# Attention values as 128-column float32r matmuls, with the mask and the row maximum in one operation

## The chip, the cores and the metric

The kernel runs on one core of one Trainium2 chip. The metric is the device time of one execution in microseconds (us). The profiler calls the engines PE (TensorE: matmuls; its weight loads are listed apart as PEld), DVE (VectorE), ACT (ScalarE), POOL (GpSimd) and SP (SyncE, which issues the large DMAs).

## The reference

One decoder layer on x of 256 tokens by 1024 features, all float32. The part that the change touches is the attention: 8 heads of 64 features, one block of 256 tokens, so that the block-sparse attention of the reference is plain causal attention.

```python
h = rmsnorm(x, norm_mix_g)
q, k, v, u_pool, gate_logits = split(h @ w_in)
q, k = rotary(rmsnorm(heads(q))), rotary(rmsnorm(heads(k)))
p = softmax(where(k_pos <= q_pos, q @ k.T * Dh ** -0.5, -1e30))
attn = p @ v
mixed = sigmoid(gates[0]) * (attn @ w_branch_attn) + sigmoid(gates[1]) * (pooled @ w_branch_pool)
x = x + mixed @ w_out
x = x + ffn(rmsnorm(x))        # up projection, causal convolution, silu(gate) * value, down projection
```

## The kernel before

**Float32 from two halves.** Nearly every product runs as three float32r matmuls. An operand is split into a high part (`high`, a ScalarE copy to float32r) and a low part (`low`, VectorE: the operand less its high part), and `mm3` (L95 to L101) multiplies high by high, high by low and low by high into one PSUM accumulator. Weights arrive as raw chunks of 128 x 2048 by DMA and are split in pieces of 128 x 1024: `next_high` and `next_low`, called by `ahead`, keep ScalarE and VectorE some pieces ahead of PE. The tiles of a split chunk are named after what they belong to: `hi_g`, `lo_g` for the gates, `bp` and `ba` for the two branch weights, `o` for the output weights.

**Order of the work.** The instructions of each engine run in the order in which the program writes them; the end of the program ties them to it. The stages, as PE sees them: q, k and v (to 38 us), the four pool inputs `ps_u`, sixteen gate tiles n = 0 to 15 (`ps_g`, 24 matmuls each), eight tiles j = 0 to 7 of the pool branch (`ps_bp`, 12 matmuls each), eight tiles of the attention branch (`ps_ba`), the output projection, and the feed-forward part from 144 us on. After each gate tile, and after every second tile of the pool branch (j = 1, 3, 5, 7), a `tick` advances a clock, and functions that were put off with `later(n, ...)` run n ticks on. Behind the tick come `ahead` and the tile's eviction by VectorE (L559 for a gate, L582 for the pool branch), so anything a tick adds on VectorE or ScalarE stands in front of the eviction.

**The attention.** It is done for pairs of heads, hp = 0 to 3, between the gate tiles. `scores` runs before the gate tiles 1, 5, 9 and 13: four float32 matmuls into a PSUM tile of three blocks of 128 columns per head (the first 128 queries with the first 128 keys, and the other 128 queries with all 256), one VectorE operation that adds the mask (L480), two reductions for the maxima (L484), one that scales them (L485), four exponentials with sums on ScalarE (L492), a reciprocal (L495), two multiplications on GpSimd (L498). Four ticks on, `weigh` transposes the weights on PE (L506) and copies them out (`pT`, L508). Four ticks later (one for the last pair) `values` multiplies: eight matmul records per pair, float32, 64 stationary columns of v each, into `ps_o` (L517); ScalarE and VectorE split the result into `ath` and `atl` (L519, L520). So the tick behind gate tile 8 runs the values of pair 0 and the transposes of pair 1; behind gate tile 12 the values of pair 1 and the transposes of pair 2; behind tile 1 of the pool branch the values of pair 2 and the transposes of pair 3; behind tile 3 the values of pair 3. Before gate tile 10 the pool maps `ps_m` run.

**Buffers.** The eight PSUM banks are four single ones (`mm`: gate tiles, branch tiles, `ps_o`) and two pairs (`ps2`: scores, transposes, pool maps). A new tile gets the slot that was given back first, and its first matmul waits for the last reader of the tile that was there. `vn` (v by token) lies in the same buffer as the tokens that the first norm reads.

Of the kernel before, what the change touches and what calls it, by code (L numbers as in the profile page):

```python
# [8 lines left out]
F32 = mybir.dt.float32  # L9
F32R = mybir.dt.float32r  # L10
AF = mybir.ActivationFunctionType
ALU = mybir.AluOpType
AX = mybir.AxisListType

P = 128
S = 256
NT = S // P
D = 1024
KD = D // P
H = 8  # L20
DH = 64
AW = H * DH
KA = AW // P
# [6 lines left out]
HALF = ROPE // 2  # L30
EPS = 1e-6
NEG = -1e30
CH = 2048


# [31 lines left out]
def hybrid_layer_kernel(ctx: ExitStack, tc: tile.TileContext, xq_d, xtok_d, par_d, wkv_d, wpg_d,  # L67
                        wpool_d, wba_d, wbp_d, wout_d, wup_d, wdn_d, out_d):
    nc = tc.nc

    const = ctx.enter_context(tc.tile_pool(name="const", bufs=1))
# [3 lines left out]
    act = ctx.enter_context(tc.tile_pool(name="act", bufs=1))  # L75
# [4 lines left out]
    tmp = mixer.enter_context(tc.tile_pool(name="tmp", bufs=2))  # L80
# [5 lines left out]
    def high(hi, src, scale=1.0):  # L86
        nc.scalar.activation(hi, src, AF.Copy, scale=scale)  # L87

    def low(lo, hi, src, scale=None):
        if scale is None:  # L90
            nc.vector.tensor_tensor(lo, src, hi.bitcast(F32), ALU.subtract)  # L91
        else:
            nc.vector.scalar_tensor_tensor(lo, src, scale, hi.bitcast(F32), ALU.mult, ALU.subtract)
# [24 lines left out]
    def load(parts=1):  # L118
# [5 lines left out]
        n = src.shape[-1]  # L124
        raws[c] = raw_p.tile([P, CH], F32, tag="raw", name=f"raw_{name}{c}")
        for i in range(parts):
# [8 lines left out]
    for c, (name, src) in enumerate(order):  # L135
        n = CH if name == "q" else src.shape[-1]
        parts = 4 if name == "q" else 2 if n == CH else 1
        pieces += [(c, slice(i * n // parts, (i + 1) * n // parts), i == 0, i == parts - 1) for i in range(parts)]
# [5 lines left out]
    at = [0, 0]  # L144
# [8 lines left out]
    def next_high():  # L153
        if at[0] < len(pieces):
# [4 lines left out]
            if first:  # L159
                moving = order[c][0] in "qkv"  # L160
                place = MOVING if moving else 0
                his[c] = whi_p.tile([P, CH + P], F32R, tag="whi", name=f"hi_{order[c][0]}{c}")[:, place:]
                place = MOVING if moving else FAR
                los[c] = wlo_p.tile([P, CH + P], F32R, tag="wlo", name=f"lo_{order[c][0]}{c}")[:, place:]
            high(his[c][:, sl], raw(c, sl))
# [13 lines left out]
    def ahead(upto=0):  # L179

        next_high()
        next_low()
        if at[1] - sum(p[0] < used[0] for p in pieces) < upto:
            next_high()
            next_low()
# [29 lines left out]
    load(2)  # L215
    load()

    vn = act.tile([P, 2 * NT, AW], F32, tag="v", name="vn")
    xtok = vn.rearrange("p (t a) b -> p t (a b)", t=NT)
    nc.sync.dma_start(out=xtok, in_=xtok_d)  # L220
    nc.sync.dma_start(out=par, in_=par_d)
    for _ in range(RAWBUFS - 2):
# [4 lines left out]
    for i in range(WARM):  # L227
# [6 lines left out]
    nc.gpsimd.memset(eps, EPS)  # L234
    mhalf = const.tile([P, H], F32, name="mhalf")
    nc.gpsimd.memset(mhalf, -0.5)
    mask = const.tile([P, 3, P], F32, name="mask")
    nc.gpsimd.memset(mask, 0.0)
    nc.gpsimd.affine_select(out=mask[:, 0:3:2, :], in_=mask[:, 0:3:2, :], compare_op=ALU.is_ge, fill=NEG,
                            base=0, pattern=[[0, 2], [-1, P]], channel_multiplier=1)  # L240
    rcnt = const.tile([P, 16], F32, name="rcnt")
    nc.gpsimd.iota(rcnt, pattern=[[1, 16]], base=1, channel_multiplier=0,
                   allow_small_or_imprecise_dtypes=True)
# [142 lines left out]
    ptq = project("q", on_q)  # L386
    ptk = project("k", on_k)

    psv = ps2.tile([P, 2, 512], F32, tag="ps2", name="ps_v")
    ptv = project("v", on_v, [psv[:, t, :] for t in range(NT)])  # L390
    for t in range(NT):
# [5 lines left out]
    def later(n, fn, *args):  # L397
        due.setdefault(clock[0] + n, []).append((fn, args))
# [43 lines left out]
    for b in range(2):  # L442
        w = chunk("p")
        for c in range(2):
            ps = feature_tile(w, c, f"u{b}{c}")
# [9 lines left out]
                    nc.gpsimd.tensor_tensor(qs[:, t, :], qs[:, t, :], mhalf[:, 0:H], ALU.pow)  # L455


    ath = act.tile([P, KA, S], F32R, tag="ath", name="ath")
    atl = act.tile([P, KA, S], F32R, tag="atl", name="atl")
    gates = xq[:, :, S:].rearrange("p k (i s) -> p k i s", s=S)  # L460

    def gate(n):
# [4 lines left out]
    TOK = (slice(0, P), slice(P, 3 * P))  # L467

    def scores(hp):
        ps = ps2.tile([P, 2, 512], F32, tag="ps2", name=f"ps_s{hp}")  # L470
        for j in range(2):
            rows = slice(j * DH, (j + 1) * DH)
            nc.tensor.matmul(ps[:, j, P:3 * P], qT[rows, hp, P:S], kT[rows, hp, :], start=True, stop=True)
            nc.tensor.matmul(ps[:, j, 0:P], qT[rows, hp, 0:P], kT[rows, hp, 0:P], start=True, stop=True)
        if hp == 0:

            for _ in range(2):
                next_high()
        sm = tmp.tile([P, 2, 3 * P], F32, tag="big", bufs=4, name=f"sm{hp}")
        nc.vector.tensor_tensor(sm, ps[:, :, 0:3 * P],  # L480
                                mask.rearrange("p a b -> p (a b)")[:, None, :].to_broadcast([P, 2, 3 * P]), ALU.add)
        mx = tmp.tile([P, 2, 2], F32, tag="mx", name=f"mx{hp}")
        for t in (1, 0):
            nc.vector.tensor_reduce(mx[:, t, :], sm[:, :, TOK[t]], axis=AX.X, op=ALU.max)  # L484
        nc.vector.scalar_tensor_tensor(mx, mx, -1.0, qs[:, :, 2 * hp:2 * hp + 2], ALU.mult, ALU.mult)  # L485
        if hp == 0:
            for _ in range(2):
                next_low()
        sums = tmp.tile([P, 2, 2], F32, tag="sums", name=f"sums{hp}")
        for j in range(2):  # L490
            for t in (1, 0):
                nc.scalar.activation(sm[:, j, TOK[t]], sm[:, j, TOK[t]], AF.Exp, bias=mx[:, t, j:j + 1],  # L492
                                     scale=qs[:, t, 2 * hp + j:2 * hp + j + 1], accum_out=sums[:, t, j:j + 1])
        rs = tmp.tile([P, 2, 2], F32, tag="rs", name=f"rs{hp}")
        nc.vector.reciprocal(rs, sums)  # L495
        for t in (1, 0):
            n = TOK[t].stop - TOK[t].start
            nc.gpsimd.tensor_tensor(sm[:, :, TOK[t]], sm[:, :, TOK[t]],  # L498
                                    rs[:, t, :, None].to_broadcast([P, 2, n]), ALU.mult)
        later(4, weigh, hp, sm)  # L500

    def weigh(hp, sm):
        pp = ps2.tile([P, 2, 512], F32, tag="ps2", name=f"ps_p{hp}")
        for j in range(2):
            for b in range(3):
                nc.tensor.transpose(pp[:, j, b * P:(b + 1) * P], sm[:, j, b * P:(b + 1) * P], ident)  # L506
        pT = tmp.tile([P, 2, 3 * P], F32, tag="big", bufs=4, name=f"pT{hp}")
        nc.scalar.activation(pT, pp[:, :, 0:3 * P], AF.Copy)  # L508
        later(1 if hp == KA - 1 else 4, values, hp, pT)

    def values(hp, pT):

        po = bank(f"ps_o{hp}")
        for b in range(2):
            for j in range(2):
                h = 2 * hp + j
                nc.tensor.matmul(po[j * DH:(j + 1) * DH, b * P:S], vn[:, b, h * DH:(h + 1) * DH],  # L517
                                 pT[:, j, 2 * b * P:(2 * b + 2 - b) * P], start=b == 0, stop=b == 1)
        high(ath[:, hp, :], po[:, 0:S])  # L519
        low(atl[:, hp, :], ath[:, hp, :], po[:, 0:S])  # L520

    waiting = list(range(KD, 2 * KD)) + list(range(KD))

# [23 lines left out]
    for n in range(2 * KD):  # L547
        if n >= FIRST and (n - FIRST) % 4 == 0:
            scores((n - FIRST) // 4)
        if n == 10:  # L550
            pool_maps()
            ahead()
        b, c = n // 2, n % 2
        if c == 0:
            w = chunk("g")
        ps = feature_tile(w, c, f"g{n}")
        tick()
        ahead(AHEAD if n % 2 else 0)
        nc.vector.tensor_tensor(gate(n), ps[:, 0:S], R1, ALU.mult)  # L559
        if n >= 2 * KD - 2:  # L560
            sigmoids(3)


    def branch(src, oph, opl, j, w):
        hi, lo = w
        ps = bank(f"ps_b{src}{j}")
        for k in range(4):
            sl = slice(k * 512 + (j % 4) * P, k * 512 + (j % 4 + 1) * P)
            mm3(ps[:, 0:S], (hi[:, sl], lo[:, sl]), (oph[:, k, :], opl[:, k, :]), k == 0, k == 3)
        return ps  # L570

    for j in range(KD):
        if j % 4 == 0:
            w = chunk("bp")
        ps = branch("p", poolh, pooll, j, w)
# [8 lines left out]
    tmp = ctx.enter_context(tc.tile_pool(name="ffn", bufs=2))  # L584
# [3 lines left out]
    for j in range(KD):  # L588
        if j % 4 == 0:
            w = chunk("ba")  # L590
        ps = branch("a", ath, atl, j, w)
        sigmoids(1)
        if j in (1, 3):
            ahead()
        nc.vector.tensor_tensor(gate(j), ps[:, 0:S], gate(j), ALU.mult)
        nc.gpsimd.tensor_tensor(gate(j), gate(j), gate(KD + j), ALU.add)
        high(mh[:, j, :], gate(j))
        if j:
            low(ml[:, j - 1, :], mh[:, j - 1, :], gate(j - 1))
# [39 lines left out]
    for b in range(4):  # L639
        w = chunk("o")  # L640
        ps = [bank(f"ps_out{b}{c}") for c in range(2)]
# [92 lines left out]
    w = chunk("up")  # L734
    ps = [bank("ps_up1_0")]
# [6 lines left out]
    for i in range(1, KF):  # L742
        if i > 1:
            w = chunk("up")
            ps = [up_tile(w, 0, i)]
# [101 lines left out]
```

## Time and profile before

| what | value |
|---|---|
| three runs | 335.17, 335.31, 335.36 us |
| span of the profiled execution, first to last instruction | 333.6 us |
| what lies around the span, against the median of the runs | 1.7 us |
| granted TensorE clock, mean | 0.998 |
| PE busy | 328.6 us (99%) |
| VectorE busy | 254.9 us (76%) |
| ScalarE busy | 202.6 us (61%) |
| GpSimd busy | 82.3 us (25%) |

The profile is of one execution. Times inside it count from its first instruction. A row of the timeline has the start, the length, the engine, the line in the kernel, the operation and what it writes and reads; in square brackets stands how long the engine was idle before it, and who ended that. The chain of waits is followed back from the last instruction; its rows have a start, a length and what ran. The lengths of matmuls overlap, so their spacing is taken from the chain or from counts in a stretch of time. A row of the stretches has the length, then each engine's busy time with its number of instructions.

### The profile page before, as it was taken

The page shows a single profiled execution, that of the slowest core. Times are in us where ns is not written, and L with a number is a line of the kernel's source. Part 1 is how long each engine was busy: PE and PEld are TensorE (multiplying, and loading weights), DVE is VectorE, ACT ScalarE, POOL GpSimd, SP SyncE. Part 2 cuts the span into 40 slices and gives each one's busy share as a digit, 9 for nine tenths or more (in the row PEclk, how much of TensorE's full clock was granted, in tenths as well). Part 3 has the DMA queues.
Part 4 walks back from the last instruction along what each step waited for, and adds up shares of the span by engine and source line. Part 5 has one row for each costly group of instructions (what it writes and reads, how often), then busy time and mean ns, then how long its engine had stood idle before and what let it go on. Part 6 is the DMA issues. An engine that isn't in the chain of part 4 may idle for free.

```text
span 333.6 us, 6696 instructions
## 1 busy us (share of the span) xinstructions
PE 328.6 (99%) x2728; PEld 319.5 (96%) x2728; DVE 254.9 (76%) x408; ACT 202.6 (61%) x326; POOL 82.3 (25%) x98
## 2 busy tenths in 40 slices
PE   8999999999999999999999999999999999999995
PEld 7888899999999999999999999999999999999995
DVE  4939979979778866877997977777777777768844
ACT  5767626645849945767766766555656464646520
POOL 1007771102404034121241212121212121221330
PEclk9999999999999999999999999999999999999999
DMA  7999763474455660763529283636454555543003
GB/s 266 422 415 205 226 271 129 157 253 149 145 210 181 218 235 2 252 210 110 209 106 358 72 328 129 252 130 252 140 240 146 233 163 216 182 198 128 0 2 126
DMA packets 11102, 63.94 MB, mean 192 GB/s; under 512 B 1472, under 2 KB 2752, under 8 KB 4032
## 3 DMA queue, kind: packets, MB, share of 16 engines
q1 hardware_dynamic: 10656, 63.39, 53.3%
q8 instruction: 21, 0.34, 0.4%
q10 hardware_dynamic: 416, 0.13, 0.3%
q14 instruction: 9, 0.07, 0.1%
HBM read 62.47 MB, written 1.05 MB: 190 GB/s over the span
## 4 chain that ended last, share of the span: by engine, by line
PE 97%; DMA 1%; ACT 0%; DVE 0%; issue 0%
PE ps_up L99 12%; PE ps_up L101 12%; PE ps_up L100 12%; PE ps_d L707 6%; PE ps_d L709 6%; PE ps_d L708 6%; PE ps_g L99 5%; PE ps_g L101 4%; PE ps_g L100 4%; PE ps_q L298 3%; PE ps_k L298 3%; PE ps_v L298 3%; PE ps_out L99 2%; PE ps_out L101 2%; PE ps_out L100 2%; DMA xq<-in_xq 1%
## 5 line engine op out<-in xcount | busy, mean ns | idle before, releaser
L101 PE MATMUL ps_up<-hhi,lo_up 128*128 128x256 f32 x352 | 97.2, 276 | 0.0
L99 PE MATMUL ps_up<-hhi,hi_up 128*128 128x256 f32 x352 | 97.2, 276 | 0.0
L100 PE MATMUL ps_up<-hlo,hi_up 128*128 128x256 f32 x352 | 97.2, 276 | 0.0
L100 PEld LDWEIGHTS ps_up<-hlo,hi_up 128*128 128x128 f32 x352 | 66.1, 188 | 0.0
L101 PEld LDWEIGHTS ps_up<-hhi,lo_up 128*128 128x128 f32 x352 | 66.1, 188 | 0.0
L99 PEld LDWEIGHTS ps_up<-hhi,hi_up 128*128 128x128 f32 x352 | 66.1, 188 | 0.0
L91 DVE TENSOR_TENSOR lo_up<-raw_up,hi_up 128x1024 fp32r<-128x1024 f32 x44 | 54.7, 1261 | 7.3 <-ACT hi_up L87 7.3
L707 PE MATMUL ps_d<-ah,hi_dn 128*128 128x256 f32 x176 | 48.6, 276 | 0.0
L708 PE MATMUL ps_d<-al,hi_dn 128*128 128x256 f32 x176 | 48.6, 276 | 0.0
L709 PE MATMUL ps_d<-ah,lo_dn 128*128 128x256 f32 x176 | 48.6, 276 | 0.0
L689 POOL TENSOR_TENSOR c_v<-c_g,c_v 128x256 f32<-128x256 f32 x22 | 16.2, 736 | 121.4 <-DVE c_v L672 121.4
L87 ACT ACTIVATE hi_up<-raw_up 128x1024 fp32r<-128x1024 f32 x44 | 44.1, 1047 | 0.0
L87 ACT ACTIVATE ah<-c_v 128x256 fp32r<-128x256 f32 x22 | 9.2, 418 | 45.6 <-POOL c_v L689 45.6
L99 PE MATMUL ps_g<-xhi,hi_g 128*128 128x256 f32 x128 | 35.9, 280 | 0.0
L100 PE MATMUL ps_g<-xlo,hi_g 128*128 128x256 f32 x128 | 35.3, 276 | 0.0
L101 PE MATMUL ps_g<-xhi,lo_g 128*128 128x256 f32 x128 | 35.3, 276 | 0.0
L707 PEld LDWEIGHTS ps_d<-ah,hi_dn 128*128 128x128 f32 x176 | 33.0, 188 | 0.0
L708 PEld LDWEIGHTS ps_d<-al,hi_dn 128*128 128x128 f32 x176 | 33.0, 188 | 0.0
L709 PEld LDWEIGHTS ps_d<-ah,lo_dn 128*128 128x128 f32 x176 | 33.0, 188 | 0.0
L91 DVE TENSOR_TENSOR lo_dn<-raw_dn,hi_dn 128x1024 fp32r<-128x1024 f32 x22 | 27.8, 1263 | 0.4 <-ACT hi_dn L87 0.4
L677 DVE TENSOR_TENSOR u_v<-ps_up,R 128x256 f32<-128x256 f32 x22 | 9.3, 421 | 20.9 <-PE ps_up L101 20.8
L714 POOL TENSOR_TENSOR al<-c_v,ah 128x256 fp32r<-128x256 f32 x22 | 22.0, 1002 | 11.6 <-ACT ah L87 11.6
(188 smaller groups left out, 794.7 us busy)
## 6 DMA issues: line engine op xcount, KB each, us to landing
raw_up<-in_wup SPq DMA_DIRECT2D x22, 1024.0 KB, 4.9
raw_dn<-in_wdn SPq DMA_DIRECT2D x11, 1024.0 KB, 4.9
raw_g<-in_wpg SPq DMA_DIRECT2D x8, 1024.0 KB, 5.9
raw_o<-in_wout SPq DMA_DIRECT2D x4, 1024.0 KB, 4.7
raw_v<-in_wkv SPq DMA_DIRECT2D x2, 1024.0 KB, 15.4
raw_p<-in_wpg SPq DMA_DIRECT2D x2, 1024.0 KB, 12.9
raw_bp<-in_wbp SPq DMA_DIRECT2D x2, 1024.0 KB, 4.8
raw_ba<-in_wba SPq DMA_DIRECT2D x2, 1024.0 KB, 4.7
```

The lines of the kernel that those rows point to most:

```text
L87: nc.scalar.activation(hi, src, AF.Copy, scale=scale)
L91: nc.vector.tensor_tensor(lo, src, hi.bitcast(F32), ALU.subtract)
L99: nc.tensor.matmul(out, sh, mh, start=start, stop=False, **kw)
L100: nc.tensor.matmul(out, sh, ml, start=False, stop=False, **kw)
L101: nc.tensor.matmul(out, sl, mh, start=False, stop=stop, **kw)
L298: nc.tensor.matmul(pt[t], sx[:, k, t * P:(t + 1) * P], wx[:, sl], start=k == 0 and sx is xhi and wx is hi, stop=k == KD - 1 and wx is lo)
L677: nc.vector.tensor_tensor(u, ps[:, 0:S], R2, ALU.mult)
L689: nc.gpsimd.tensor_tensor(uc[1], g[1], uc[1], ALU.mult)
L707: nc.tensor.matmul(o, hi[:, sl], acch[i], start=first, stop=False, skip_group_check=True)
L708: nc.tensor.matmul(o, hi[:, sl], accl[i], start=False, stop=False, skip_group_check=True)
L709: nc.tensor.matmul(o, lo[:, sl], acch[i], start=False, stop=i == KF - 1, skip_group_check=True)
L714: nc.gpsimd.tensor_tensor(accl[i], act_i, acch[i].bitcast(F32), ALU.subtract)
```

## The change

**Values.** v is split once into high and low parts in float32r (`part_values`, before gate tile 7): for each pair of heads `vv` holds the four blocks high and low of the first head, low and high of the second. The transposed weights are split too: `ph` by ScalarE out of PSUM, `pl` by VectorE, one tick after the transposes (at once for the last pair). Eight float32r matmuls per pair then have 128 stationary columns, the high and the low part of one head side by side, and add up all four products; a head's two halves of PSUM are summed afterwards: ScalarE copies one half out, and `joined`, one tick later (at once for the last pair), adds the other on VectorE, and splits the sum by a ScalarE copy and a subtraction on GpSimd. The copies and sums of all pairs use one buffer. `vn` lies in the buffer that the split attention result takes later.

**Scores.** Four fused operations (add the mask, maximum along the row) take the place of the mask addition and the two reductions. The mask shrinks to two blocks.

```diff
+    vn = act.tile([P, NT, AW], F32, tag="ath", name="vn")
+    vv = act.tile([P, NT, KA, 4, DH], F32R, tag="v", name="vv")
...
+    def part_values():
+        for t in range(NT):
+            v4 = vn[:, t, :].rearrange("p (q j d) -> p q j d", j=2, d=DH)
+            high(vv[:, t, :, 0:4:3, :], v4)
+            for j in range(2):
+                low(vv[:, t, :, 1 + j, :], vv[:, t, :, 3 * j, :], v4[:, :, j, :])
+        heads.extend(act.tile([P, KA, S], F32R, tag=tag, name=tag) for tag in ("ath", "atl"))
...
-        nc.vector.tensor_tensor(sm, ps[:, :, 0:3 * P],
-                                mask.rearrange("p a b -> p (a b)")[:, None, :].to_broadcast([P, 2, 3 * P]), ALU.add)
         mx = tmp.tile([P, 2, 2], F32, tag="mx", name=f"mx{hp}")
-        for t in (1, 0):
-            nc.vector.tensor_reduce(mx[:, t, :], sm[:, :, TOK[t]], axis=AX.X, op=ALU.max)
+        masks = (mask[:, 1, :], mask.rearrange("p a b -> p (a b)"))
+        for j in range(2):
+            for t in (1, 0):
+                nc.vector.tensor_tensor_reduce(sm[:, j, TOK[t]], ps[:, j, TOK[t]], masks[t], 1.0, LOWEST,
+                                               ALU.add, ALU.max, mx[:, t, j:j + 1])
...
-        pT = tmp.tile([P, 2, 3 * P], F32, tag="big", bufs=4, name=f"pT{hp}")
-        nc.scalar.activation(pT, pp[:, :, 0:3 * P], AF.Copy)
-        later(1 if hp == KA - 1 else 4, values, hp, pT)
+        ph = tmp.tile([P, 2, 3 * P], F32R, tag="big", bufs=4, name=f"ph{hp}")
+        pl = tmp.tile([P, 2, 3 * P], F32R, tag="big", bufs=4, name=f"pl{hp}")
+        high(ph, pp[:, :, 0:3 * P])
+        if hp == KA - 1:
+            low(pl, ph, pp[:, :, 0:3 * P])
+        else:
+            later(1, low, pl, ph, pp[:, :, 0:3 * P])
+        later(1 if hp == KA - 1 else 4, values, hp, ph, pl)
...
-        for b in range(2):
-            for j in range(2):
-                h = 2 * hp + j
-                nc.tensor.matmul(po[j * DH:(j + 1) * DH, b * P:S], vn[:, b, h * DH:(h + 1) * DH],
-                                 pT[:, j, 2 * b * P:(2 * b + 2 - b) * P], start=b == 0, stop=b == 1)
-        high(ath[:, hp, :], po[:, 0:S])
-        low(atl[:, hp, :], ath[:, hp, :], po[:, 0:S])
+        for j in range(2):
+            for p in (ph, pl):
+                for b in range(2):
+                    nc.tensor.matmul(po[:, j * S + b * P:(j + 1) * S],
+                                     vv[:, b, hp, 2 * j:2 * j + 2, :].rearrange("p a d -> p (a d)"),
+                                     p[:, j, 2 * b * P:(2 * b + 2 - b) * P], start=j == 0 and p is ph and b == 0,
+                                     stop=p is pl and b == 1, skip_group_check=True)
+        sums = tmp.tile([P, 2, S], F32, tag="q2", bufs=1, name=f"at{hp}")
+        for j in range(2):
+            nc.scalar.activation(sums[halves[j], 0, :], po[halves[1 - j], j * S:(j + 1) * S], AF.Copy)
+        if hp == KA - 1:
+            joined(hp, po, sums)
+        else:
+            later(1, joined, hp, po, sums)
+
+    def joined(hp, po, sums):
+        for j in range(2):
+            nc.vector.tensor_tensor(sums[halves[j], 1, :], po[halves[j], j * S:(j + 1) * S], sums[halves[j], 0, :], ALU.add)
+        high(heads[0][:, hp, :], sums[:, 1, :])
+        nc.gpsimd.tensor_tensor(heads[1][:, hp, :], sums[:, 1, :], heads[0][:, hp, :].bitcast(F32), ALU.subtract)
...
+        if n == 7:
+            part_values()
```

More of the change, by code (lines that the diff above doesn't have):

```diff
@@ L32 @@
 NEG = -1e30
+LOWEST = -3e38
 CH = 2048
@@ L216, in hybrid_layer_kernel @@
     load()
-    vn = act.tile([P, 2 * NT, AW], F32, tag="v", name="vn")
-    xtok = vn.rearrange("p (t a) b -> p t (a b)", t=NT)
+    xtok = act.tile([P, NT, D], F32, tag="v", name="xtok")
     nc.sync.dma_start(out=xtok, in_=xtok_d)
@@ L236, in hybrid_layer_kernel @@
     nc.gpsimd.memset(mhalf, -0.5)
-    mask = const.tile([P, 3, P], F32, name="mask")
+    mask = const.tile([P, 2, P], F32, name="mask")
     nc.gpsimd.memset(mask, 0.0)
-    nc.gpsimd.affine_select(out=mask[:, 0:3:2, :], in_=mask[:, 0:3:2, :], compare_op=ALU.is_ge, fill=NEG,
-                            base=0, pattern=[[0, 2], [-1, P]], channel_multiplier=1)
+    nc.gpsimd.affine_select(out=mask[:, 1, :], in_=mask[:, 1, :], compare_op=ALU.is_ge, fill=NEG,
+                            base=0, pattern=[[-1, P]], channel_multiplier=1)
     rcnt = const.tile([P, 16], F32, name="rcnt")
@@ L455, in hybrid_layer_kernel @@
                     nc.gpsimd.tensor_tensor(qs[:, t, :], qs[:, t, :], mhalf[:, 0:H], ALU.pow)
-    ath = act.tile([P, KA, S], F32R, tag="ath", name="ath")
-    atl = act.tile([P, KA, S], F32R, tag="atl", name="atl")
+    heads = []
+    def part_values():
[5 more added lines that the diff above has]
+        heads.extend(act.tile([P, KA, S], F32R, tag=tag, name=tag) for tag in ("ath", "atl"))
     gates = xq[:, :, S:].rearrange("p k (i s) -> p k i s", s=S)
@@ L506, in weigh @@
                 nc.tensor.transpose(pp[:, j, b * P:(b + 1) * P], sm[:, j, b * P:(b + 1) * P], ident)
-        pT = tmp.tile([P, 2, 3 * P], F32, tag="big", bufs=4, name=f"pT{hp}")
-        nc.scalar.activation(pT, pp[:, :, 0:3 * P], AF.Copy)
-        later(1 if hp == KA - 1 else 4, values, hp, pT)
-    def values(hp, pT):
-        po = bank(f"ps_o{hp}")
-        for b in range(2):
-            for j in range(2):
-                h = 2 * hp + j
-                nc.tensor.matmul(po[j * DH:(j + 1) * DH, b * P:S], vn[:, b, h * DH:(h + 1) * DH],
-                                 pT[:, j, 2 * b * P:(2 * b + 2 - b) * P], start=b == 0, stop=b == 1)
-        high(ath[:, hp, :], po[:, 0:S])
-        low(atl[:, hp, :], ath[:, hp, :], po[:, 0:S])
+        ph = tmp.tile([P, 2, 3 * P], F32R, tag="big", bufs=4, name=f"ph{hp}")
@@ new lines, in weigh, with values @@
+        pl = tmp.tile([P, 2, 3 * P], F32R, tag="big", bufs=4, name=f"pl{hp}")
[5 more added lines that the diff above has]
+        later(1 if hp == KA - 1 else 4, values, hp, ph, pl)
+    halves = (slice(0, DH), slice(DH, P))
+    def values(hp, ph, pl):
+        po = bank(f"ps_o{hp}")
+        for j in range(2):
[12 more added lines that the diff above has]
+            later(1, joined, hp, po, sums)
@@ L590, in hybrid_layer_kernel @@
             w = chunk("ba")
-        ps = branch("a", ath, atl, j, w)
+        ps = branch("a", heads[0], heads[1], j, w)
         sigmoids(1)
```

## The prediction

> **What bounds the kernel now.** I read the page's busy times first, then the chain that ended last, then the list of what PE waited for, and last the three queues (PE, VectorE, ScalarE) around the four head pairs. All times are us.
>
> ```profile
> span 333.6 us, 6696 instructions
> PE 328.6 (99%) x2728; PEld 319.5 (96%) x2728; DVE 254.9 (76%) x408; ACT 202.6 (61%) x326; POOL 82.3 (25%) x98
> PE 97%; DMA 1%; ACT 0%; DVE 0%; issue 0%
> ...
> PE ps_warm L228 <- DVE ones L196: 1.1, 1, 1.1
> PE ps_q L298 <- ACT hi_q L87: 0.4, 1, 0.4
> ...
> 55.00:65.00 10.00, 10.00 (x90) 10.00 (x89) 9.75 (x20) 6.10 (x14) 1.64 (x2) 1.00 0.27 71
> 104.00:117.00 13.00, 13.00 (x116) 12.11 (x115) 10.99 (x18) 12.99 (x25) 0.64 (x1) 1.00 0.74 253
> ```
>
> PE is the bound, and after its first 6 us it waits for nothing: its only two waits are at the start. So every microsecond in which PE is made to wait later is added to the end, and nothing after it can give it back. The windows also show where that is easy: from 104 to 117, the stage of the pool branch (`ps_bp`), ScalarE is busy 12.99 of 13.00 and VectorE 10.99, against 6.10 and 9.75 of 10.00 in the gate stage (this one is columns PE, PEld, DVE, ACT, POOL, clock, DMA). The clock is full in both. The 90 matmuls of 10.00 us in the gate stage, nearly all float32r with 256 moving columns, are 0.111 apart; twelve of them, one tile of the pool branch, take some 1.38 (four such tiles lie between 111.96 and 117.5 below).
>
> The four head pairs in the chain of waits (start, length):
>
> ```profile
> 65.74 0.66 PE ps_p L506 x6
> ...
> 78.37 0.80 PE ps_o L517 x8
> 79.17 0.81 PE ps_p L506 x6
> ...
> 107.62 0.81 PE ps_p L506 x6
> ...
> 111.16 0.80 PE ps_o L517 x8
> 111.96 0.32 PE ps_bp L99
> ...
> L99 PE MATMUL ps_ba<-ath,hi_ba x32: 276/276/276, 117.5 to 128.0; 128*128 128x256 f32 x32
> ```
>
> **PE's own price.** Out go 0.80 per pair for the values; in come eight float32r matmuls, four of 256 columns at 0.113 (0.45) and four of 128. For those the trace has no row. Lower bound: half of the 256-column spacing, 0.055. Upper: that spacing itself, 0.113. Nearest in size are the transposes, six of 128 columns in 0.66, so 0.11 each; I take that: 0.45 + 0.44 = 0.89. The transposes after a values block take 0.81 instead of 0.66, and the tile after the last one 0.32 instead of 0.11; I count both extras, 0.15 three times and 0.2, as gone with the half-width tiles. That is 4 x 0.09 more and 0.65 less: 0.3 gained, between 0.2 and 1.2.
>
> **Mask and maximum.** The row form of each:
>
> ```profile
> L484 DVE TENSOR_REDUCE mx<-sm x8: 407/548/687, 58.8 to 97.9; 128x2 f32<-128x512 f32 x4, 128x2 f32<-128x256 f32 x4
> L480 DVE TENSOR_TENSOR sm<-ps_s,mask x4: 944/946/947, 57.8 to 96.3; 128x768 f32<-128x768 f32 x4
> ...
> 56.45 2.94 ACT L87 ACTIVATE hi_g<-raw_g 128x1024 fp32r<-128x1024 f32 x3
> 60.11 0.60 ACT L492 ACTIVATE sm<-sm,mx,qs 128x256 f32<-128x256 f32 x1 [0.72 <-DVE mx L485]
> ...
> 75.42 0.39 DVE L559 TENSOR_TENSOR xq<-ps_g,R 128x256 f32<-128x256 f32 x1
> 75.73 1.50 DVE L91 TENSOR_TENSOR lo_pool<-raw_pool,hi_pool 128x512 fp32r<-128x512 f32 x1
> 77.16 0.41 DVE L559 TENSOR_TENSOR xq<-ps_g,R 128x256 f32<-128x256 f32 x1
> ...
> 81.44 0.95 DVE L480 TENSOR_TENSOR sm<-ps_s,mask 128x768 f32<-128x768 f32 x1
> ...
> 85.99 0.18 DVE L495 RECIPROCAL rs<-sums 128x4 f32<-128x4 f32 x1 [2.36 <-ACT sm L492]
> ...
> L99 PEld LDWEIGHTS ps_m<-poolh,hi_pool x4: 188/188/188, 83.5 to 84.5; 128*128 128x128 f32 x4
> ```
>
> Before: 0.95 + 0.69 + 0.41 for a pair. After: four fused operations. None is in the trace. Lower bound: a plain operation of the size, 256 elements in about 0.33 of queue time (75.42 to 75.73), and 0.20 for 128 by the slope to the mask's 768 elements: 2 x 0.53, and 0.1 before the result is read, 1.18. Upper: no cheaper than now, 2.03 of queue time. One pass over the same elements is nearest to the plain operation, so 1.18: 0.85 saved per pair.
>
> **VectorE up to the tenth gate tile.** New are pl (128x768, as long as the mask's 0.95, of which 0.87 holds up the queue) and four `low` of v (4 x 0.33 = 1.34). They stand before and behind the eviction at 77.16. Saved by then are 0.85 at pair 1 and 0.75 at pair 0, where ScalarE, busy to 59.4, takes over as the later one (its exponentials now start at 60.11). So that eviction starts at 77.16 - 1.6 + 0.87 = 76.4, and v's last part is ready at 76.4 + 0.33 + 1.34 = 78.1; PE wants it at 78.37. It costs nothing, by a margin of 0.2; without it, each 0.1 more per fused operation, eight of them by then, costs PE 0.6 to 0.8 here. ScalarE's two new copies (0.69 each by the old copy of v) fall in its idle time. The pool maps (ps_m) at 83.5 need a ps2 slot: the one given back first is that of pair 2's scores, whose masking starts at 81.44 or earlier and is through 1.2 later, 82.6 at the latest: again nothing, by 0.9. The smaller mask and vn's other place cost nothing: GpSimd builds the one while it waits for the first norms, and the other tile is empty then.
>
> **The pool branch, where it lands.** The end of the last scores on PE, then VectorE, ScalarE and GpSimd now:
>
> ```profile
> 95.52 0.22 PE ps_s L474 x4
> ...
> 94.54 0.42 DVE L91 TENSOR_TENSOR atl<-ps_o,ath 128x256 fp32r<-128x256 f32 x1 [0.78 <-ACT ath L87]
> ...
> 96.35 0.95 DVE L480 TENSOR_TENSOR sm<-ps_s,mask 128x768 f32<-128x768 f32 x1
> ...
> 98.63 0.60 ACT L492 ACTIVATE sm<-sm,mx,qs 128x256 f32<-128x256 f32 x1 [1.96 <-DVE mx L485]
> ...
> 108.39 0.49 ACT L527 ACTIVATE xq<-xq,par 128x256 f32<-128x256 f32 x1
> 108.79 0.36 ACT L87 ACTIVATE ath<-ps_o 128x256 fp32r<-128x256 f32 x1
> 109.06 0.79 ACT L508 ACTIVATE pT<-ps_p 128x768 f32<-128x768 f32 x1
> ...
> 107.52 0.42 DVE L582 TENSOR_TENSOR xq<-ps_bp,xq 128x256 f32<-128x256 f32 x1
> 109.19 0.42 DVE L91 TENSOR_TENSOR atl<-ps_o,ath 128x256 fp32r<-128x256 f32 x1 [1.25 <-ACT ath L87]
> 109.53 1.22 DVE L91 TENSOR_TENSOR lo_ba<-raw_ba,hi_ba 128x1024 fp32r<-128x1024 f32 x1
> 110.66 0.42 DVE L582 TENSOR_TENSOR xq<-ps_bp,xq 128x256 f32<-128x256 f32 x1
> 111.00 1.22 DVE L91 TENSOR_TENSOR lo_ba<-raw_ba,hi_ba 128x1024 fp32r<-128x1024 f32 x1
> ...
> L714 POOL TENSOR_TENSOR al<-c_v,ah 128x256 fp32r<-128x256 f32 x22 | 22.0, 1002 | 11.6 <-ACT ah L87 11.6
> L689 POOL TENSOR_TENSOR c_v<-c_g,c_v 128x256 f32<-128x256 f32 x22 | 16.2, 736 | 121.4 <-DVE c_v L672 121.4
> ```
>
> Pair 2's values and pair 3's transposes are both done in the tick after bp1. ScalarE comes there about 0.2 earlier than now. The exponentials of pair 3 start 1.4 earlier: without atl and its idle 0.78 VectorE can mask when the scores end, 95.8 instead of 96.35, and saves 0.85. But behind the exponentials ScalarE now waits for the reciprocal and the adds of pair 1 (0.1 + 0.8) before their `high` (0.3), 1.2. From 108.6: two copies instead of one (2 x 0.26), ph to 109.9; VectorE stands since 107.9 with pl at its head, which now waits for ph: 109.97 to 110.84; behind it lo_ba (1.13, the two rows' distance) and only then the eviction of bp1, done at 112.4 instead of 111.08.
>
> The four mm banks at that moment hold bp1, o2, bp2, bp3. Now o3 takes o2's bank, free once atl at 109.19 is done. After the change o2's is held until `joined`, one tick later, behind the eviction of bp2. So o3 must wait for bp1's: **112.45 instead of 111.16**. It ends at 113.35. bp4 needs bp2's bank: 112.3 + 1.13 + 0.42 = 113.85, so **113.9 instead of 111.96**, 1.95 late. Next is `joined` of pairs 2 and 3, which share one `at` buffer: adds 113.8 to 114.6 (2 x 0.33, and 0.08 each for a half that starts elsewhere), `high` to 115.05 (0.42), GpSimd's subtract to 116.1 (1.00), then the copies of pair 3 to 116.8, its adds to 117.75. bp5 has o2's bank; bp6 waits for o3's: 117.8 instead of 116.75 (113.9 + two tiles + 0.1), another 1.05. From there the banks come in time, and the branch `ps_ba` starts at 120.5 instead of 117.5: **3.0 late**.
>
> PE's 0.3 is lost in this: o3 starts when VectorE has evicted bp1, however early PE is there. Sum: 333.6 + 3.0 = 336.6 of span; the median of the runs shown, 335.31, is 1.7 over the span, so **338.3**. Unknowns: GpSimd's subtract at 0.74 (its other row) takes 0.26 off; copies of 64 partitions cheaper by 0.06 each, 0.2 off; ScalarE not 0.2 early, 0.2 on; 0.05 more per fused operation, 0.5 on. Its own range is 337.6 to 339.2.
>
> **Rivals.** A: the fused operation takes a second instruction on VectorE for its maximum. For: ScalarE's exponentials with sums are each followed by one,
>
> ```profile
> 60.62 0.19 ACT L492 ACTIVATION_READ_ACCUMULATOR sm<-sm,mx,qs 128x1 f32 x1
> 60.71 0.48 ACT L492 ACTIVATE sm<-sm,mx,qs 128x128 f32<-128x128 f32 x1
> ```
>
> of 0.19, of which 0.09 holds up the queue. With 0.09 on each, v's last part is 0.7 later at pair 0, 0.5 past PE's need, and the chain above is up to 0.6 later (four of them at pair 3, and what is left of pair 1's): 339.4; with the whole 0.19 on each, twice that, 340.5. Against: VectorE's reductions now show no second instruction. [...] B: the fused operation is no cheaper than mask and reduce: the 1.6 saved up to pair 0's values and the 0.85 at pair 3 are gone, 1.4 at the one place and 0.85 to 1.5 at the other on top of 3.0: 341.0. C: the pool maps get pair 1's ps2 slot, which waits for pl behind the reciprocal at 85.99 (then 84.7), the adds and pl's 0.95: 86.5 instead of 83.5, 3.0 more, 341.3; against it, the order in which the slots come back. D: only o3's bank is late, by 1.3, and VectorE, which idles here now, catches up behind it: 336.6. E, the other side: PE never waits. It decides at the eviction of bp1: if VectorE ends it by 111.1, as now, o3 is not held and only PE's own price is left, 335.0 (334.1 at the lower bound of the 128-column price, 335.1 at the upper). For it: VectorE is idle 1.25 before atl, and that hides part of pl. Against: to come in time pl must start at 108.7, and the transposes it reads end at 108.43, with ph's 0.79 between. [...]
>
> **How the numbers follow.** Forecast 0.55, A 0.17, B 0.06, C 0.03, D 0.09, E and what lies between it and D 0.10. A difference under 0.2%, 0.67, can't be told from none in this kernel. Everything but E is slower by more; of E I give 0.05 to over 0.67 faster, the rest to no difference: faster 0.05, same 0.07, slower 0.88. The range takes in the forecast, D and most of A: 336.4 to 340.8.
>
> **What would show it.** PE waits for VectorE's eviction L582 before the fourth values block (1.3) and before two tiles of the pool branch (0.6 and 1.0), and nowhere else; `ps_ba` starts near 120.5; the mask operation's four instructions take 0.42 and 0.28; pl of pair 3 stands after an idle VectorE that ended on ScalarE. I am wrong if PE shows no waits after 6 us, or if they stand at 78 or 84.

## The result and the profile after

The changed kernel takes 339.42 us (median of 4 runs, 338.95 to 339.67) against 335.34 for the kernel before (4 runs): 1.012 times as long, with a 95% interval of 1.0106 to 1.0135. The forecast was 338.3, so the direction holds and 1.1 us are missing from it. The profiled execution took 339.67 with a span of 337.9, 4.3 more than before.

The lines of the changed kernel are shifted: the evictions of the pool branch, L582 before, are L614; the values, L517, are L534; the `low` of L91 is L92. Its page (span, busy times, and in 40 slices PE's busy tenths and the granted clock) and the list of what PE waited for (us in total, times, longest):

```profile
span 337.9 us, 6743 instructions
PE 331.1 (98%) x2728; PEld 323.4 (96%) x2728; DVE 257.8 (76%) x440; ACT 207.0 (61%) x336; POOL 84.4 (25%) x102
PE   8999999999999799999999999999999999999995
PEclk9999999999999899999999999999999999999999
```

```profile
PE ps_o L534 <- DVE xq L614: 2.1, 1, 2.1
PE ps_warm L228 <- DVE ones L197: 1.1, 1, 1.1
PE ps_bp L100 <- DVE xq L614: 0.3, 1, 0.3
```

Two waits are new, both on VectorE's eviction of a pool-branch tile: 2.1 before a values block (the fourth, by the timeline below) and 0.3 before the tile behind it. That makes 2.4 of the 4.3. The rest is in the page's last line shown: the fourteenth slice (109.8 to 118.3) shows clock 8 where before every slice shows 9. Cut finer, in windows of 1 us (columns PE, PEld, DVE, ACT, POOL, granted clock, DMA share, GB/s):

```profile
114.00:115.00 1.00, 0.73 (x7) 0.58 (x6) 0.99 (x4) 0.00 (x0) 0.00 (x0) 1.00 0.49 180
115.00:116.00 1.00, 1.00 (x8) 1.00 (x7) 0.29 (x1) 0.42 (x1) 0.18 (x1) 0.66 0.93 393
116.00:117.00 1.00, 1.00 (x7) 1.00 (x6) 0.00 (x0) 0.41 (x2) 0.55 (x1) 0.50 0.97 410
117.00:118.00 1.00, 1.00 (x6) 1.00 (x6) 0.55 (x2) 0.35 (x1) 0.00 (x0) 0.50 0.01 0
118.00:119.00 1.00, 1.00 (x7) 1.00 (x7) 0.97 (x3) 0.67 (x2) 0.18 (x1) 0.63 0.00 0
119.00:120.00 1.00, 1.00 (x11) 1.00 (x10) 1.00 (x2) 1.00 (x3) 1.00 (x1) 1.00 0.00 0
```

PE is busy from 115 to 119 and yet gets through 6 to 8 matmuls in a microsecond where it does 11 of these at 119: the granted clock is at 0.50 from 116 to 118. What is missing to 1.00 adds up to 0.34 + 0.50 + 0.50 + 0.37 = 1.71 us, which is 3.4 us at half clock. In this execution it begins 2.1 us after the wait has ended.

What VectorE, ScalarE and GpSimd did around the wait, in the timeline (start, length; in brackets the idle time before, and what ended it):

```profile
107.61 0.42 DVE L614 TENSOR_TENSOR xq<-ps_bp,xq 128x256 f32<-128x256 f32 x1
110.64 0.96 DVE L92 TENSOR_TENSOR pl<-ps_p,ph 128x768 fp32r<-128x768 f32 x1 [2.60 <-ACT ph L88]
111.51 1.22 DVE L92 TENSOR_TENSOR lo_ba<-raw_ba,hi_ba 128x1024 fp32r<-128x1024 f32 x1
112.64 0.42 DVE L614 TENSOR_TENSOR xq<-ps_bp,xq 128x256 f32<-128x256 f32 x1
112.98 1.22 DVE L92 TENSOR_TENSOR lo_ba<-raw_ba,hi_ba 128x1024 fp32r<-128x1024 f32 x1
114.11 0.42 DVE L614 TENSOR_TENSOR xq<-ps_bp,xq 128x256 f32<-128x256 f32 x1
114.44 0.84 DVE L548 TENSOR_TENSOR at<-ps_o,at 64x256 f32<-64x256 f32 x2
117.44 0.86 DVE L548 TENSOR_TENSOR at<-ps_o,at 64x256 f32<-64x256 f32 x2 [2.15 <-POOL atl L550]
...
109.00 0.77 ACT L540 ACTIVATE at<-ps_o 64x256 f32<-64x256 f32 x2
109.79 0.81 ACT L88 ACTIVATE ph<-ps_p 128x768 fp32r<-128x768 f32 x1
...
113.20 0.41 PE L534 MATMUL ps_o<-ph,vv 128*128 128x256 f32 x2 [2.06 <-DVE xq L614]
114.58 0.39 PE L100 MATMUL ps_bp<-poolh,hi_bp 128*128 128x256 f32 x1 [0.27 <-DVE xq L614]
```

This is the chain of the forecast: VectorE stands idle for 2.60 with `pl` at its head, then come `pl`, `lo_ba`, the eviction at 112.64, and at its end PE starts the fourth values block.

Summed: 2.06 + 0.27 of waits and 1.71 of half clock are 4.04. The stage from the first matmul of `ps_bp` (104.0) to the first of `ps_ba` (121.8) takes 17.83, before 13.51, which is 4.32 more; the 0.3 that is left belongs to the two breaks: a wait is counted from the end of the matmul before it, 0.28 after its start, while the next one otherwise starts 0.11 after it. By the starts of the same matmuls in both traces, the stages ahead of it and behind it last the same: 25.64 from the first values block to the first of `ps_bp`, 10.88 from the first of `ps_ba` to the first of `ps_out`.

### The profile page after: what moved, and what is told of

Read it like the earlier page. It is cut to its first block, busy times and chain, and to the rows that moved or that the text cites. A ratio compares the mean times of both kernels' runs of the same rounds, so it can differ in the third digit from the quotient of the medians.

```text
span 337.9 us, 6743 instructions
## 1 busy us (share of the span) xinstructions
PE 331.1 (98%) x2728; PEld 323.4 (96%) x2728; DVE 257.8 (76%) x440; ACT 207.0 (61%) x336; POOL 84.4 (25%) x102
## 3 DMA queue, kind: packets, MB, share of 16 engines
HBM read 62.47 MB, written 1.05 MB: 188 GB/s over the span
## 4 chain that ended last, share of the span: by engine, by line
PE 97%; DVE 1%; issue 0%; ACT 0%
PE ps_up L100 12%; PE ps_up L101 12%; PE ps_up L102 12%; PE ps_d L739 6%; PE ps_d L740 6%; PE ps_d L741 6%; PE ps_g L100 5%; PE ps_g L102 4%; PE ps_g L101 4%; PE ps_q L298 3%; PE ps_k L298 3%; PE ps_v L298 3%; PE ps_out L101 2%; PE ps_out L102 2%; PE ps_out L100 2%; PE ps_warm L228 1%
## 5 line engine op out<-in xcount | busy, mean ns | idle before, releaser
L92 DVE TENSOR_TENSOR lo_up<-raw_up,hi_up 128x1024 fp32r<-128x1024 f32 x44 | 55.0, 1268 | 7.3 <-ACT hi_up L88 7.3
L92 DVE TENSOR_TENSOR lo_dn<-raw_dn,hi_dn 128x1024 fp32r<-128x1024 f32 x22 | 27.8, 1264 | 0.4 <-ACT hi_dn L88 0.4
```

## The experiments

Theory: everything lost comes from the order of VectorE and ScalarE around the fourth pair, which makes PE wait 2.1 us for a bank; the half clock is a consequence of that wait. Rivals: the fused operation, TensorE's own new instructions, the one `at` buffer, or the new work of 64 partitions beside the matmuls is at fault.

The results in one table. "Stage" is the time from the first matmul of `ps_bp` to the first of `ps_ba` in the profiled execution, "half clock" the length at 0.50 that the windows give.

| kernel | PE's waits in the stage | half clock | stage | median | ratio to before, 95% |
|---|---|---|---|---|---|
| before | none | none | 13.51 | 335.3 | 1 |
| changed | 2.1, 0.3 | 3.4 | 17.83 | 339.42 | 1.0106 to 1.0135 |
| e1_fused | none | none | 13.51 | 335.41 | 0.9993 to 1.0011 |
| e2_values | 3.2, 0.2 | 3.4 | 18.73 | 340.74 | 1.0148 to 1.0186 |
| e3_o3pair | 0.3, 0.6, 1.2 | none | 16.35 | 338.39 | 1.0076 to 1.0104 |
| e4_relief | 0.4 | none | 14.24 | 336.45 | 1.0022 to 1.0045 |
| e5_at2 | 2.1, 0.3 | 3.4 | 17.78 | 339.50 | 1.0110 to 1.0141 |
| e6_pl_late | 0.3, 0.6, 0.8 | none | 15.93 | 337.88 | 1.0057 to 1.0088 |
| e7_gap4 | 0.9 | none | 14.63 | 336.30 | 1.0020 to 1.0045 |
| e7_gap7 | 2.3 | 3.4 | 17.51 | 339.34 | 1.0099 to 1.0130 |
| e7_gap9 | 3.2 | 6.8 | 19.53 | 341.02 | 1.0124 to 1.0181 |
| e8_relief2 | none | none | 13.50 | 335.50 | 0.9992 to 1.0009 |

**The two parts of the change, each alone.** `e1_fused` is the kernel before with

```diff
-        nc.vector.tensor_tensor(sm, ps[:, :, 0:3 * P], <mask, broadcast>, ALU.add)
-        for t in (1, 0):
-            nc.vector.tensor_reduce(mx[:, t, :], sm[:, :, TOK[t]], axis=AX.X, op=ALU.max)
+        for j in range(2):
+            for t in (1, 0):
+                nc.vector.tensor_tensor_reduce(sm[:, j, TOK[t]], ps[:, j, TOK[t]], masks[t], 1.0, LOWEST,
+                                               ALU.add, ALU.max, mx[:, t, j:j + 1])
```

> The kernel before with the second part of the change alone: mask and maximum in one operation, the smaller mask; the values stay as they were. Theory (TensorE sets the end and waits for nothing, the loss comes from the values part): VectorE loses some 0.85 us of work per pair, TensorE notices nothing, 335.3 us, within 0.3. Rival (the fused operation is itself what costs, through its second instruction for the maximum): 0.5 to 1 us slower than before.

Measured 335.41, no difference, and no wait after the first 6 us. `e2_values` is the changed kernel with the same lines turned back.

> The kernel before with the first part of the change alone: the values as float32r with v's two parts side by side and the weights split, the mask and the maximum in two operations as before. Theory (the order of VectorE around the fourth pair costs everything, and the fused operation only takes VectorE's work from places where it is covered): the same 2.1 us wait ahead of the fourth values block and the same 3.4 us of half clock, v's last part ready by 78.0 where TensorE wants it at 78.3, 339.4, within 0.5. Rival (without the 0.85 us per pair that the fused operation saves, v's parts and the fourth pair come late): waits at 78 and before the last tiles of the pool branch, 340.3 to 341.5.

Measured 340.74 (340.33 to 340.87, and one execution of 342.07 at a mean clock of 0.989), 1.3 more than the whole change. The waits at 78 that the rival wanted aren't there, but my theory is wrong too in holding that the fused operation is worth nothing. The exponentials of the fourth pair start at 98.73, in the changed kernel at 97.25, and what follows on ScalarE stands later too, in the timeline of `e2_values`:

```profile
98.73 0.60 ACT L501 ACTIVATE sm<-sm,mx,qs 128x256 f32<-128x256 f32 x1 [1.55 <-DVE mx L494]
...
111.27 0.81 ACT L88 ACTIVATE ph<-ps_p 128x768 fp32r<-128x768 f32 x1
...
112.11 0.96 DVE L92 TENSOR_TENSOR pl<-ps_p,ph 128x768 fp32r<-128x768 f32 x1 [2.60 <-ACT ph L88]
```

and in its list of waits:

```profile
PE ps_o L533 <- DVE xq L613: 3.2, 1, 3.2
```

Against the changed kernel's `ph` at 109.79 that is 1.5 later (0.3 of it from a later start of the whole program), and PE's wait grows from 2.1 to 3.2. So the fused operation is worth nothing in the kernel before and some 1.3 us beside the new values, because it shortens the chain that ends in this wait.

**The bank, the buffer and VectorE's order.** Three kernels move one thing each in the changed kernel. `e3_o3pair`:

```diff
-        po = bank(f"ps_o{hp}")
+        if hp == KA - 1:
+            po = ps2.tile([P, 2, 512], F32, tag="ps2", name=f"ps_o{hp}")[:, 0, :]
+        else:
+            po = bank(f"ps_o{hp}")
```

> The changed kernel, but the fourth pair's values go to the free double bank instead of one of the four banks. [...] Rival (the wait is for the weights, whatever the bank): the 2.1 us wait stays, 339.4.

`e5_at2`:

```diff
-        sums = tmp.tile([P, 2, S], F32, tag="q2", bufs=1, name=f"at{hp}")
+        sums = tmp.tile([P, 2, S], F32, tag="q2" if hp % 2 == 0 else "at", bufs=1, name=f"at{hp}")
```

> The changed kernel, but the sums of the second and fourth pair have a buffer of their own, so that the fourth pair's copies need not wait for GpSimd's subtraction of the third's. Theory (at half clock TensorE comes to the seventh pool-branch tile at 119.4, after its bank is free at 117.9): the earlier bank changes nothing, 339.4, within 0.3. Rival (the prediction's step, 1.05 us for this bank, is part of what was measured): 338.4 to 338.8.

`e6_pl_late`:

```diff
         if hp == KA - 1:
-            low(pl, ph, pp[:, :, 0:3 * P])
+            late.append((pl, ph, pp[:, :, 0:3 * P]))
...
         nc.vector.tensor_tensor(gate(KD + j), ps[:, 0:S], gate(KD + j), ALU.mult)
+        if j == 1:
+            low(*late.pop())
```

> The changed kernel with one instruction moved: VectorE makes the low part of the fourth pair's weights behind the eviction of the second pool-branch tile instead of ahead of it. Theory (VectorE's order is the cause): that tile is evicted by 110.0, the fourth values block waits only for its weights, 0.3, the fifth tile of the pool branch 0.6 for the third's eviction, the seventh 1.0 for the one buffer of the sums; 1.9 in all, in pieces, so the clock stays full: 337.3. Rival (the low part of the weights, 0.95 us of VectorE, is in the way wherever it stands): 338.5 to 339.4.

What PE waited for, first in `e3_o3pair`, then in `e6_pl_late`:

```profile
PE ps_bp L100 <- DVE xq L617: 1.8, 2, 1.2
...
PE ps_o L537 <- DVE pl L92: 0.3, 1, 0.3
```

```profile
PE ps_bp L100 <- DVE at L549: 0.8, 1, 0.8
PE ps_bp L100 <- DVE xq L615: 0.6, 1, 0.6
PE ps_o L535 <- DVE pl L92: 0.3, 1, 0.3
```

In both the 2.1 us wait is gone: the wait was for the bank, and the weights alone hold the block up by 0.3. What comes instead stands ahead of the fourth block and two later tiles, in `e3_o3pair` 0.33, 0.56 before the fifth tile and 1.24 before the eighth, in `e6_pl_late` 0.33, 0.64 before the fifth and 0.84 before the seventh, and the clock is full (1.00 from 108 to 122 in both). Yet both kernels are slower than the times I had for them, `e3_o3pair` by 0.4 (338.0) and `e6_pl_late` by 0.6 (337.3). `e3_o3pair` has 2.1 us of waits in three pieces, as much as the changed kernel's longest, and is 1.0 faster (338.39 against 339.42). The pieces still cost more than their own length: the stage is 2.8 longer than before, some 0.2 beyond each recorded wait, and its `ps_ba` stage is another 0.4 longer (11.29 against 10.88). `e5_at2` changes nothing, so the `at` buffer's bank, the third term of the forecast, was not part of the 4.3: counted back from `ps_ba` at 121.8 by two tiles of 1.38, PE came to the seventh tile at 119.0, while its bank was free at 118.3, when the additions from 117.44 were done. In `e6_pl_late`, with the clock full, this wait for the additions is there, the 0.8 in its list.

**All of it put right.** `e4_relief` joins the three edits and puts `ph` of the fourth pair ahead of the third pair's two copies on ScalarE.

```diff
         high(ph, pp[:, :, 0:3 * P])
+        if hp == KA - 1:
+            copies(*held.pop())
...
-        for j in range(2):
-            nc.scalar.activation(sums[halves[j], 0, :], po[halves[1 - j], j * S:(j + 1) * S], AF.Copy)
+        if hp == KA - 2:
+            held.append((po, sums))
+        else:
+            copies(po, sums)
```

> The changed kernel with four things moved around the fourth pair, nothing computed differently: its values go to the free double bank; ScalarE makes the high part of its weights ahead of the third pair's two copies; VectorE makes the low part behind the eviction of the second pool-branch tile instead of ahead of it; the sums of the second and fourth pair have a buffer of their own. Theory (all 4.3 us come from the order of VectorE and ScalarE here, none from TensorE's own price): TensorE waits nowhere after 6 us, the clock stays full, 335.3, within 0.5. Rival (the eight half-width matmuls or the copies of 64 partitions cost TensorE something by themselves): 336 to 338.

Measured 336.45, which lies in the rival's range: three quarters of the loss is gone, not all; the stage is 0.7 longer than before, and `ps_ba` behind it 0.4, where one matmul (119.55) starts 0.29 behind the one before it instead of 0.11. One wait of 0.4 is left before the eighth tile; its bank's eviction stands on VectorE behind the fourth pair's additions, which stand idle:

```profile
115.02 0.86 DVE L562 TENSOR_TENSOR at<-ps_o,at 64x256 f32<-64x256 f32 x2 [1.34 <-POOL atl L564]
115.91 0.42 DVE L628 TENSOR_TENSOR xq<-ps_bp,xq 128x256 f32<-128x256 f32 x1
...
113.72 0.42 ACT L88 ACTIVATE ath<-at 128x256 fp32r<-128x256 f32 x1 [0.64 <-DVE at L562]
114.16 0.77 ACT L558 ACTIVATE at<-ps_o 64x256 f32<-64x256 f32 x2
```

The releaser named is GpSimd, but by the order of ScalarE it is the fourth pair's copies that the additions read, and these stand behind `ath` of the third pair. `e8_relief2` lets the copies go first:

```diff
         if hp == KA - 1:
+            joined(*pair2.pop())
             joined(hp, po, sums)
+        elif hp == KA - 2:
+            pair2.append((hp, po, sums))
```

> The kernel with four things moved around the fourth pair, and a fifth: the fourth pair's copies stand on ScalarE ahead of the third pair's high part, and both pairs' additions follow each other on VectorE, so that the eviction of the fourth pool-branch tile need not wait 1.3 us for them. Theory (what was left there, 0.4 before the eighth tile and some 0.3 behind it, is this one wait): no wait of TensorE over 0.1 after 6 us, 335.3 or up to 0.2 less, since TensorE's own work is 0.04 a pair shorter. Rival (the remaining microsecond belongs to TensorE's own instructions): 336.2 or more.

From its page, and then the whole list of what PE waited for:

```profile
span 333.9 us, 6745 instructions
PE   8999999999999999999999999999999999999995
```

```profile
PE ps_warm L228 <- DVE ones L197: 1.1, 1, 1.1
```

335.50, a ratio of 1.0001: nothing was computed differently from the changed kernel, and its whole loss is gone. So neither TensorE's own instructions nor the work of 64 partitions costs anything that can be measured here. Nor do they bring anything: in the best order found here the change ties with the kernel before. No kernel of these beats it.

**The clock by itself.** The kernel before, with n additions on VectorE ahead of one eviction, and nothing of the change:

```diff
         sigmoids(1)
+        if j == 1:
+            for i in range(9):      # e7_gap9; 7 and 4 in the others
+                nc.vector.tensor_tensor(idle, xT[:, 0, :], xT[:, 1, :], ALU.add)
         nc.vector.tensor_tensor(gate(KD + j), ps[:, 0:S], gate(KD + j), ALU.mult)
```

> The kernel before, with nine additions of 256 columns on VectorE ahead of the eviction of the second pool-branch tile, some 3.0 us, whose result nobody reads; nothing of the change is in it. The slack there is 0.9, so TensorE must wait some 2.1 us ahead of the fifth tile. Theory (a wait of this length by itself brings half the clock for 3.4 us afterwards, which costs 1.7): 335.3 + 2.1 + 1.7 = 339.1. Rival (the slow matmuls of the changed kernel come from its own new work, copies and additions of 64 partitions beside them): the clock stays full, 337.4.

The additions, all into one tile, took 0.46 each instead of 0.33, so the wait became 3.2. The timeline, the list of waits and the windows of `e7_gap9`:

```profile
110.57 4.10 DVE L585 TENSOR_TENSOR idle<-xq 128x256 f32<-128x256 f32 x9
```

```profile
PE ps_bp L99 <- DVE xq L586: 3.2, 1, 3.2
```

```profile
114.00:116.00 2.00, 0.95 (x4) 0.95 (x5) 1.97 (x4) 2.00 (x5) 0.00 (x0) 0.51 0.41 172
116.00:118.00 2.00, 2.00 (x12) 2.00 (x11) 2.00 (x5) 1.01 (x3) 0.00 (x0) 0.50 0.00 0
118.00:120.00 2.00, 2.00 (x11) 2.00 (x11) 1.72 (x3) 0.00 (x0) 0.00 (x0) 0.50 0.25 53
120.00:122.00 2.00, 2.00 (x15) 2.00 (x15) 0.42 (x1) 0.00 (x0) 0.00 (x0) 0.78 0.99 406
```

The clock falls without anything of the change in the kernel: the rival is out. What is missing is (0.49 + 0.50 + 0.50 + 0.22) x 2 = 3.42, so 6.8 us at half, twice the length of the other cases; it begins at 114.04, 1.0 us before PE's wait ends. Of its four executions three took 340.87 to 341.23 and one 338.65, which is 335.3 + 3.2 with almost nothing added: in that one the clock (0.998 in the mean, against 0.990 to 0.994) did not fall noticeably.

> The kernel before, with four additions on VectorE ahead of the eviction of the second pool-branch tile, 0.46 each by the run with nine, 1.8 together; the slack of 0.92 taken off, TensorE waits 0.9 us. Theory (a wait that is short against the 3.4 us for which the clock stays at half has no aftermath): 335.3 + 0.9 = 336.2, the clock full in every run. Rival (any wait of TensorE brings the clock down): 336.2 + 1.7 = 337.9.

> The same with seven additions, 3.2 us together, so a wait of 2.3 us, close to that of the changed kernel. [...] Rival (the length alone decides): all four alike, within 0.4.

With 0.9 the clock stays full (1.00 in the windows, 0.999 to 1.0 in the mean of its six executions) and the time is 336.30, as expected. With 2.3 all four executions lie between 338.99 and 339.45: 1.5 to 1.9 above the 337.5 that the wait alone gives, every time. I had expected the half clock in some of the four only; they are alike, 0.46 apart, close to the rival's 0.4. Over all runs: a single wait of 2.1 or 2.3 brought the half clock in all twelve executions (the changed kernel, `e5_at2`, `e7_gap7`; the windows of three show it, and the others by mean clocks of 0.993 to 0.995), one of 3.2 in the values kernel and here in seven of eight (0.989 to 0.995), and none of 0.9 or less did, nor pieces of 0.3, 0.6 and 1.2 within 8 us (mean clocks of 0.998 to 1.0). Where the half clock begins isn't tied to the wait: by the windows 2.1 us after its end in the changed kernel, 1.2 in `e5_at2` with the same wait, 0.45 in `e7_gap7`, and in `e7_gap9` before its end.

By the sums of what is missing to 1.00, the half clock lasted 3.42 us in the changed kernel, `e5_at2`, `e7_gap7` and `e2_values`, and 6.84 in `e7_gap9`. How long a single wait must be for it remains open between the 0.9 that never brought it and the 2.1 that always did. What let one execution with 3.2 escape is not shown.

## Why the prediction was right, and where its sizes were off

**The place and the mechanism** hold: PE waits for L614 ahead of the fourth values block because o2's bank is still held and bp1's is evicted late, behind `pl` and `lo_ba`. `e3_o3pair` shows that it is the bank, `e6_pl_late` that it is VectorE's order, and `e8_relief2` that nothing else is in it.

**o3, forecast 1.3 late, was 2.1 late.** The step that failed is the start of `ph`: 109.79 instead of 109.1. ScalarE came to the copies at 109.00, not 108.6: it was 0.1 later than before, not 0.2 earlier, since the second pair's additions and `high` behind the fourth pair's exponentials held it from 99.40 to 100.87, 1.5 instead of 1.2, and the copies start 0.5 behind the operation in front of them, not 0.4. And the copies of 64 partitions took 0.39 each instead of 0.26. From there on every step has its forecast length and is 0.7 late.

**bp4, forecast 1.95 late, was 2.7 late** (114.58): the same 0.7, nothing new. Its own wait is 0.27 instead of 0.6, because the wait is counted from the end of the block's last matmul, 1.1 after the block's start; the sum took 0.9.

**bp6, another 1.05: did not happen.** The step left out the clock. At half clock for 3.4 us, 1.71 lost, PE came late enough for the bank; `e5_at2` shows that the buffer no longer mattered, and `e6_pl_late`, with the clock full, has this wait with 0.8. Without the fall PE would have come to bp6 at 114.58 + 2.76 = 117.3 and waited to 118.3, so of the 1.71 only about 0.7 stands on top of the forecast's own chain; with the 0.7 of `ph` and 0.3 less for GpSimd's subtraction (0.73, not 1.00) that is the 1.1 by which the forecast fell short. The 0.08 that the forecast adds for a half that starts elsewhere was my estimate, and no row of the trace before has such an operation; the two additions hold VectorE's queue for 0.88 (117.44 to 118.32), forecast 0.82.

**PE's own price, forecast 0.3 gained, is next to nothing.** In the chain of the changed kernel:

```profile
93.36 0.88 PE ps_o L534 x8
94.23 0.67 PE ps_p L516 x6
```

The block is 0.88 (forecast 0.89) and by the chain the transposes lose their extra (0.81 to 0.67), yet the stretch from the first values block to the pool branch takes 25.64 in both kernels. By the starts of their matmuls, block and transposes together take 1.64 instead of 1.61; what is gained, 0.09, lies ahead of the block, whose first matmul now starts 0.11 behind the gate tile's last one instead of 0.20. Counted from the gate tile ahead of the first block on, the stretch to the pool branch is 36.69 instead of 36.76: 0.07 gained in two pairs.

**Mask and maximum, 0.85 saved per pair,** holds. For the fourth pair:

```profile
95.82 0.42 DVE L493 CUSTOM_DVE_ANT_0 sm<-ps_s,mask 128x256 f32<-128x256 f32 x1 [0.34 <-PE ps_s L483]
96.17 0.09 DVE L493 DVE_READ_ACCUMULATOR2_ANT mx<- 128x1 f32 x1
96.17 0.29 DVE L493 CUSTOM_DVE_ANT_0 sm<-ps_s,mask 128x128 f32<-128x128 f32 x1
...
97.06 0.16 DVE L495 SCALAR_TENSOR_TENSOR mx<-mx,qs 128x4 f32<-128x4 f32 x1
```

1.24 from the first to the read-out, forecast 1.18. Rival A's second instruction is there, 0.09 long, but the next operation starts with it at 96.17, so it takes no time of the queue that shows: at most the 0.06 that all four are over the forecast. Rival A fell for that reason alone; that its 339.4 is what was measured is chance.

**v's parts, margin 0.2, had 1.9.** They were ready at 76.4:

```profile
74.00 0.68 DVE L92 TENSOR_TENSOR lo_pool<-raw_pool,hi_pool 128x512 fp32r<-128x512 f32 x1
...
74.93 1.51 DVE L92 TENSOR_TENSOR vv<-vn,vv 128x256 fp32r<-128x256 f32 x4
```

`lo_pool` takes 0.68 instead of 1.50, and VectorE was a microsecond earlier already ahead of the first pair, which I did not foresee. That microsecond is luck: VectorE waits there for the DMA into `R`, until 43.39 before and 42.35 here, and until 42.0 to 43.4 over all twelve traces, with the change and without. Right in its sign, this step was off by 1.7. Rival B (waits at 78) and C (the pool maps' slot) show no wait at all; D had the catch-up wrong, since bp4 waited as well; E would have needed the eviction by 111.1, and `e8_relief2`, where it starts at 110.02, is what E looks like.

## What to carry to other kernels

An instruction put ahead of an eviction on an in-order engine costs what it waits for as well as what it lasts, here 2.60 and 0.87: follow the PSUM bank behind that eviction to the matmul that wants it, and put the eviction first. Where TensorE is the bound, a wait can cost more than it lasts: here one of 2.3 us cost 4.1, with 3.4 us at a clock of 0.50 behind it (`e7_gap7`), and 2.1 in three pieces 3.1 (`e3_o3pair`). And work saved on an engine that isn't the bound is worth nothing until something puts that engine on the chain: the fused operation was worth 0 alone and 1.3 beside the new values.

## What was not expected of the hardware

- A single wait of TensorE of 2.1 to 2.3 us was followed by 3.4 us at a granted clock of 0.50, which cost 1.7 us, in the three traces that have one; the times and mean clocks of all twelve executions agree. After a wait of 0.9 us the clock stayed full (`e7_gap4`, 1.00 in every window from 108 to 122).
- The accumulator read behind a fused operation is an instruction of 0.07 to 0.09 us in the trace and starts at the same instant as the next operation.
- GpSimd's subtraction of 256 columns took 0.73 us with VectorE idle, and more than twice as long beside VectorE's `lo_ba` at 118.67. In all seven traces with the new values the three subtractions that start just behind a `low` of 128x1024 on VectorE take 1.66 to 1.76, and the third pair's, with no `low` beside it, 0.73 or 0.74; no run takes a `low` away to test it. In the timeline of the changed kernel:

```profile
115.81 0.73 POOL L550 TENSOR_TENSOR atl<-at,ath 128x256 fp32r<-128x256 f32 x1 [12.59 <-ACT ath L88]
118.82 1.66 POOL L550 TENSOR_TENSOR atl<-at,ath 128x256 fp32r<-128x256 f32 x1 [2.27 <-ACT ath L88]
```
